# A large network on one core: merge gates sent through DRAM, an attention head's scores moved ahead of splits, and recurrent rows gated in two halves

## The chip, the cores and the metric

The kernel runs on one core of one Trainium2 chip. A core has TensorE (matmuls and transposes; PE in the profile, with weight loads listed as PEld), VectorE (DVE), ScalarE (ACT), GpSimd (POOL) and SyncE (SP), and DMA engines that the queues of SP, ACT and POOL feed. Each engine works through its own instructions in order. The metric is the time of one execution in microseconds, the median of three runs.

## The reference

A sequence of 512 tokens of width 1024 goes through two blocks. The first has two layers: a dilated sliding-window attention (three groups of windows, eight heads each, whose outputs are mixed by their log-sum-exp) and a gated linear recurrence, each followed by a convolutional feed-forward layer. The second block has two layers with three branches each, merged by gates:

```python
# one head of the first attention: three groups g, mixed by alpha
o = jnp.sum(jax.nn.softmax(jnp.stack(lses), axis=0)[..., None] * jnp.stack(outs), axis=0)
# recurrent layer
gate = jax.nn.gelu(gb, approximate=True)
_, hs = lax.associative_scan(_lru_combine, (a, b), axis=1)
return (hs * gate) @ w_out
# second block, per layer
h = _rmsnorm(x, norm_g[l]); z = h @ w_in[l]
o_a = nsa(...) * silu(nsa_silu); o_b = fox(...) * silu(fox_silu); o_m = memory(...) * silu(mem_silu)
g = jax.nn.sigmoid(merge_g).reshape(B, T, 3, D)
u = g[:, :, 0] * (o_a @ w_branch_a) + g[:, :, 1] * (o_b @ w_branch_b) + g[:, :, 2] * (o_m @ w_branch_m)
x = x + u @ w_out[l]
```

Here nsa is an attention with a compressed, a selected and a windowed part, fox an attention with forget gates, and memory a cross-attention to 256 memory rows.

## The kernel before

Every number is fp32. A matrix operand is split into a high and a low part (a cast on ACT, then a subtraction on DVE: `split`, L204), and a product is three matmuls, high x high, high x low, low x high (`mm3`, L45 to L47). Weights come by `wunit`: a load on SP's queue into one of two `ws` tiles, then a split into one of four pairs `wh`, `wl`. PSUM banks are handed out by tag: three `acc`, two `sc`, two `tr`, one `pv`.

The kernel is written in a framework in which each tile belongs to a tag with a fixed number of buffers; its scheduler orders each engine's instructions, in general by program order among those that are ready. `issue_after(ins)` (wrapped by `behind`) queues what is written inside it behind `ins`, on the engine of `ins` alone.

First attention (`dilated_attention`): for each of eight heads, six feature blocks of the query/key projection are computed (orders 1 and 0 of the tokens for different groups), scores, exponentials, a pair of statistics per order (`W`). The two orders exchange statistics through DRAM: L112 writes this order's, L113 reads the other's. `normalize` combines them (DVE, ACT, then POOL scales the rows), and `values` transposes the scaled rows (tags PA, PB; L143, L154) and multiplies them with the values. For the last head these two run inside `hold`, between the first seven eighths and the last eighth of the output projection's first half (`tm`). The projection's left operand is the split of oT, one split for each head.

Recurrent layer (`lru_layer`): `LRU_STEPS` writes out an order. An integer n is `front(n)` (convolution, gate matrices, tanh for rows 2n and 2n+1), a range is `recur` (the decay exponentials and the scan for these rows), and each "v" copies one of eight raw gate blocks from its bank to a tile on DVE. At the end, every row m gets its Gelu (from the raw copy, or straight from the bank for the rest), is multiplied with it and split for the output projection.

Second layers (`second_layer`): memory, nsa and fox are generators; `weave` runs one of them and, after the steps listed in `PLANS`, calls a filler generator once. nsa and fox have 40 steps each, memory 20. The filler is `branch`: for each of eight column blocks m a gate (24 matmuls, in two calls, then a tanh into a tile `mt`) and a product o @ w_branch (12 matmuls), multiplied with (1 + tanh) into u by DVE and, for the second and third branch, added to u by POOL (L1043, L1046, L1047). The gate of m + 1 comes before the product of m. The tag `st` has seven buffers of [128, 2048] fp32, which hold keys, values, queries and the two u tiles.

Of the kernel before, what the change touches and what calls it, by code (L numbers as in the profile page):

```python
# [28 lines left out]
SEC_BUFS = {"st": 7, "ws": 2, "w": 4, "o": 6, "P": 5, "pt": 4, "zc": 3, "hst": 4, "fox_t": 4, "of": 2, "rt": 2, "sl": 2, "mt": 2, "cst": 2, "ct": 2}  # L29
LRU_BUFS = 24  # L30
NORMALIZE_AFTER, VALUES_AFTER = 5, 6
LRU_STEPS = (0, 1, 2, range(4), "v", 3, range(4, 8), "vvv")
PLANS = ((16,),
         (8, 13, 13, 14, 15, 18, 19, 19, 22, 22, 25, 26, 26, 27, 27, 28, 28, 29, 29, 35, 35, 37, 38, 39),
         (1, 5, 5, 8, 8, 10, 12, 15, 16, 17, 19, 21, 32, 32, 34, 35, 38))
# [24 lines left out]
class DilatedHead:  # L60
# [23 lines left out]
    def scores(self, qk, order):  # L84
        n, nc = self.n, self.n.nc
        own = self.W[:, order, 0]
        ps = None
        for t in range(NT):
            ts = slice(t * 128, (t + 1) * 128)
            P = self.rows(order, t)  # L90
            N = P.shape[-1]
            if order:

                S = n.bank("sc").rearrange("p (g u c) -> p u g c", g=2, u=2)
                for g in (1, 2):
                    q = qk[g]
                    nc.tensor.matmul(S[:, :, g - 1], q[:, 0, ts], q[:, 2:4, ts], start=True, stop=False)
                    nc.tensor.matmul(S[:, 0, g - 1], q[:, 1, ts], q[:, 2, ts], start=False, stop=True)
                two = lambda x: x.rearrange("p (g c) -> p g c", g=2)
                nc.vector.tensor_tensor(two(P), S[:, 1], two(self.bias[:, 256:512]), op=OP.add)  # L100
                S, bias, P3 = S[:, 0], two(P), two(P)
            else:
                if t % 2 == 0:
                    ps = n.bank("sc")
                S = ps[:, t % 2 * 256:t % 2 * 256 + N]
                q, ks = qk[0], slice((t + 1) * 128 - N, (t + 1) * 128)
                mm3(nc, S, q[:, 0, ts], q[:, 1, ts], q[:, 2, ks], q[:, 3, ks], True, True)
# [61 lines left out]
class Net:  # L169
# [287 lines left out]
    def dilated_attention(self, qkv, oT):  # L457
# [54 lines left out]
        a.scores(qk, 0)  # L512
# [6 lines left out]
        return last  # L519
# [26 lines left out]
    def attn_layer(self, g_next, nxt):  # L546
        i, tc = self.i, self.tc
        with tc.tile_pool(name="attO", bufs=1) as self.op, tc.tile_pool(name="attA", bufs=2) as self.ap:
# [4 lines left out]
            last = self.dilated_attention(self.attn_qkv(self.h), oT)  # L553
# [135 lines left out]
    def lru_layer(self, lin, g_next, nxt):  # L689
        nc, i, tc = self.nc, self.i, self.tc  # L690
        with tc.tile_pool(name="lru", bufs=1) as lp:
# [63 lines left out]
            raw = 0  # L755
            for step in LRU_STEPS:
                if isinstance(step, int):
                    front(step)
                elif isinstance(step, str):
                    for e in step:  # L760
                        (nc.scalar.copy if e == "a" else nc.vector.tensor_copy)(gate[:, raw], next(lin))
                        raw += 1
                else:
                    last_y = recur(step)
            for m in range(KD):
                x, g = xs[m // 2], gate[:, m]
                ps = g if m < raw else next(lin)
                with self.tc.issue_after(last_y.ins):
                    nc.scalar.activation(g, ps, AF.Gelu_apprx_tanh)  # L769
                nc.vector.tensor_tensor(hs[m], hs[m], g, op=OP.mult)  # L770
                self.split(x[0][:, m % 2], x[1][:, m % 2], hs[m])
# [137 lines left out]
    def pv(self, ps, first, last, v, pts, half):  # L909
# [3 lines left out]
        for j in range(nj):  # L913
            lo = 128 if j == nj - 1 else 0
            for u, p in enumerate(pts):
                nc.tensor.matmul(ps[:, lo:256], v(j), p[:, j, lo:], start=first and j == 0 and u == 0, stop=last and j == nj - 1 and u == 1)  # L916
# [40 lines left out]
    def second_layer(self, l, z2):  # L957
        nc, i, tc = self.nc, self.i, self.tc
        w_in, h = i["w_in_2"][l], self.h
        with tc.tile_pool(name=f"sec{l}", bufs=1) as self.lp:  # L960
            lp = self.lp
            u, o_m, o_a, o_b = [], [], [], []
            br = [self.branch(l, h, o, i[f"w_branch_{x}_2"][l], b, u) for o, x, b in ((o_m, "m", 2), (o_a, "a", 0), (o_b, "b", 1))]
            self.weave(self.memory(l, h, w_in, z2, o_m), br[0], PLANS[0])
            self.weave(self.nsa(l, h, w_in, o_a), itertools.chain(br[0], br[1]), PLANS[1])
            self.weave(br[0])
            self.weave(self.fox(l, h, w_in, o_b), itertools.chain(br[1], br[2]), PLANS[2])
            self.weave(br[1])
            self.weave(br[2])
# [38 lines left out]
    def branch(self, l, h, o, w, b, u):  # L1008

        nc = self.nc  # L1010
        kt = 4
        wv = w.rearrange("(k p) c -> p k c", p=128)
        first = not u
        ts = []

        wg = self.i["w_in_2"][l].rearrange("(k p) c -> p k c", p=128)

        def gate(m):
# [9 lines left out]
            ts.append(t)  # L1028
            yield

        yield from gate(0)
        for m in range(KD):
            if m + 1 < KD:
                yield from gate(m + 1)
# [507 lines left out]
```

## Time and profile before

| | |
|---|---|
| median of three runs (2843.86 to 2845.45) | 2844.17 us |
| the profiled execution | 2847.33 us |
| its span, first to last instruction | 2845.2 us |
| TensorE busy | 2752.4 us, 14493 matmuls |
| DVE busy | 1655.0 us |
| ACT busy | 1285.5 us |
| POOL busy | 509.2 us |
| mean granted clock of TensorE | 0.988 |
| DMA | 288.52 MB, 101 GB/s from and to HBM over the span |

Times in views count from the span's start. A row of windows gives an engine's busy time in a stretch; the rest of the stretch it was idle. PEclk is the granted clock of TensorE as a share of full speed; it has two levels, 1.0 (2.4 GHz) and 0.5 (1.2 GHz), and a value between them is a mean over the stretch.

### The profile page before, as it was taken

What the parts mean: (1) busy time and instruction counts of PE and PEld (TensorE: products, weight loads), DVE (VectorE), ACT (ScalarE), POOL (GpSimd) and SP (SyncE); (2) the same over time, 40 slices, a digit from 0 to 9 for tenths busy, and PEclk for the clock granted to TensorE, in tenths of its full rate; (3) what the DMA queues carried; (4) which work ended last, traced back from release to release, by engine and by line L of the source; (5) the groups of instructions that cost most, each with busy time, mean ns of one, the idle gap of its engine ahead of it and who ended that gap; (6) DMA issues with size and microseconds to landing.
All of it is one profiled execution on the core that took longest, in us unless ns stands there. A gap on an engine that the chain in (4) does not pass through costs nothing.

```text
span 2845.2 us, 39405 instructions
## 1 busy us (share of the span) xinstructions
PE 2752.4 (97%) x14493; PEld 2338.7 (82%) x14493; DVE 1655.0 (58%) x3306; ACT 1285.5 (45%) x2518; POOL 509.2 (18%) x682
## 2 busy tenths in 40 slices
PE   7999999799999998999998999999999899999999
PEld 6788888688888887888887898789878798788987
DVE  3245555555542678555425687776744677777753
ACT  3234344344432465444323554666533554665542
POOL 0001101111100000111001242333320242333420
PEclk9999999899999999999999999999999999999999
DMA  5553443333332343433323424122234423113233
GB/s 172 171 169 86 104 94 86 118 111 97 97 126 96 112 122 108 126 96 97 126 97 114 125 74 109 38 54 75 71 93 141 137 70 109 34 46 84 71 93 107
DMA packets 386071, 288.52 MB, mean 101 GB/s; under 512 B 33576, under 2 KB 339496, under 8 KB 385880
## 3 DMA queue, kind: packets, MB, share of 16 engines
q1 hardware_dynamic: 376752, 268.94, 32.9%
q10 hardware_dynamic: 9128, 17.07, 1.6%
q8 instruction: 115, 1.88, 0.3%
q14 instruction: 76, 0.62, 0.1%
HBM read 266.86 MB, written 21.20 MB: 101 GB/s over the span
## 4 chain that ended last, share of the span: by engine, by line
PE 82%; DVE 8%; DMA 4%; ACT 3%; issue 2%; POOL 1%; SPq 0%; ACTq 0%; DVEq 0%; POOLq 0%
PE acc L45 20%; PE acc L46 20%; PE acc L47 20%; PE tr L856 2%; PE sc L45 2%; PE sc L46 2%; PE sc L47 2%; DVE wl L204 2%; PE pv L916 2%; PE tr L45 2%; PE tr L47 1%; PE tr L46 1%; PE pv L46 1%; PE pv L47 1%; DMA ws<-in_attn_w_qkv_dram 1%
## 5 line engine op out<-in xcount | busy, mean ns | idle before, releaser
L204 DVE TENSOR_TENSOR wl<-ws,wh 128x1024 fp32r<-128x1024 f32 (+2 forms) x476 | 563.9, 1186 | 686.8 <-ACT wh L204 680.8
L204 ACT CAST wh<-ws 128x1024 fp32r<-128x1024 f32 (+2 forms) x476 | 469.5, 987 | 819.7 <-PE acc L46 303.6
L45 PE MATMUL acc<-hH,wh 128*128 128x512 f32 (+1 forms) x1928 | 742.3, 386 | 12.2 <-ACT gate L769 6.2
L46 PE MATMUL acc<-hL,wh 128*128 128x512 f32 (+1 forms) x1928 | 741.3, 385 | 1.5 <-DVE hL L204 1.2
L47 PE MATMUL acc<-hH,wl 128*128 128x512 f32 (+1 forms) x1928 | 739.5, 384 | 1.0 <-DVE wl L204 1.0
L45 PEld LDWEIGHTS acc<-hH,wh 128*128 128x128 f32 x1928 | 363.3, 189 | 83.6 <-ACT gate L769 6.6
L47 PEld LDWEIGHTS acc<-hH,wl 128*128 128x128 f32 x1928 | 363.9, 189 | 69.2 <-DVE wl L204 1.5
L46 PEld LDWEIGHTS acc<-hL,wh 128*128 128x128 f32 x1928 | 364.1, 189 | 68.4 <-DVE hL L204 2.5
L45 PE MATMUL acc<-wh,hH 128*128 128x256 f32 (+3 forms) x864 | 267.3, 312 | 5.4 <-ACT hH L204 4.1
L46 PE MATMUL acc<-wl,hH 128*128 128x256 f32 (+3 forms) x864 | 266.9, 310 | 2.3 <-DVE wl L204 2.3
L47 PE MATMUL acc<-wh,hL 128*128 128x256 f32 (+3 forms) x864 | 264.9, 309 | 0.1
L45 PEld LDWEIGHTS acc<-wh,hH 128*128 128x128 f32 x864 | 165.6, 192 | 14.5 <-ACT hH L204 4.5
L46 PEld LDWEIGHTS acc<-wl,hH 128*128 128x128 f32 x864 | 165.7, 192 | 11.9 <-DVE wl L204 3.7
L47 PEld LDWEIGHTS acc<-wh,hL 128*128 128x128 f32 x864 | 165.3, 191 | 7.4 <-DVE hL L204 0.4
L645 POOL TENSOR_TENSOR cv<-cv 128x512 f32<-128x512 f32 x48 | 62.0, 1292 | 465.1 <-DVE cv L582 448.4
L582 DVE SCALAR_TENSOR_TENSOR cv<-acc,cw,cv 128x511 f32<-128x511 f32 (+1 forms) x192 | 142.5, 746 | 3.2
L856 PE MATMUL tr<-ident,P 128*128 128x128 f32 x720 | 123.3, 277 | 10.7 <-DVE pt L204 5.2
L817 POOL TENSOR_TENSOR hst<-hst,mhalf 128x4 f32<-128x4 f32 (+2 forms) x90 | 91.0, 1017 | 223.5 <-DVE hst L816 221.7
L889 ACT ACTIVATE P<-P,soft 128x128 f32<-128x128 f32 (+1 forms) x192 | 108.1, 563 | 49.9 <-DVE soft L888 45.7
L888 DVE CUSTOM_DVE_ANT_0 P<-sc,causal 128x128 f32<-128x128 f32 (+1 forms) x192 | 92.9, 486 | 45.8 <-PE tr L856 31.5
L891 POOL TENSOR_SCALAR P<-P,soft,ngate 128x128 f32<-128x128 f32 (+3 forms) x128 | 83.9, 658 | 153.6 <-DVE soft L890 117.5
L204 DVE TENSOR_TENSOR pt<-tr,pt 128x128 fp32r<-128x128 f32 (+2 forms) x224 | 104.1, 474 | 11.8 <-ACT pt L204 10.4
(452 smaller groups left out, 4770.1 us busy)
## 6 DMA issues: line engine op xcount, KB each, us to landing
ws<-in_w_in_dram SPq DMA_DIRECT2D x116, 512.0 KB
ws<-in_ffn_w_up_dram SPq DMA_DIRECT2D x96, 512.0 KB
ws<-in_attn_w_qkv_dram SPq DMA_DIRECT2D x72, 512.0 KB
ws<-in_ffn_w_down_dram SPq DMA_DIRECT2D x48, 512.0 KB
x<-x ACTq DMA_DIRECT2D x16, 512.0 KB
ws<-in_lru_w_in_dram SPq DMA_DIRECT2D x16, 512.0 KB
ws<-in_w_mem_kv_dram SPq DMA_DIRECT2D x16, 512.0 KB
ws<-in_w_out_dram SPq DMA_DIRECT2D x16, 512.0 KB
```

Source lines behind the costliest of these rows:

```text
L45: nc.tensor.matmul(out, lh, rh, start=start, stop=False)
L46: nc.tensor.matmul(out, lh, rl, start=False, stop=False)
L47: return nc.tensor.matmul(out, ll, rh, start=False, stop=stop)
L204: return nc.scalar.copy(hi, src), (eng or nc.vector).tensor_tensor(lo, src, hi.bitcast(F32), op=OP.subtract)
L582: nc.vector.scalar_tensor_tensor(dst[:, s:], ps[:, :T - s], cw(taps - 1 - s), dst[:, s:], op0=OP.mult, op1=OP.add)
L645: nc.gpsimd.tensor_tensor(g, g, v, op=OP.mult)
L817: nc.gpsimd.tensor_tensor(st[:, 1], st[:, 0], self.mhalf[:rows, :nh], op=OP.pow)
L856: self.nc.tensor.transpose(ps[:, a * 128:(a + 1) * 128], s, self.ident)
L888: nc.vector.tensor_tensor_reduce(out=P, in0=S, in1=self.causal[:, 512 - n:512], scale=-1.0, scalar=BIG, op0=OP.add, op1=OP.min, accum_out=m)
L889: nc.scalar.activation(P, P, AF.Exp, bias=m, scale=-1.0, accum_out=s)
L891: nc.gpsimd.tensor_scalar(P, P, r, mult, op0=OP.mult, op1=OP.mult)
L916: nc.tensor.matmul(ps[:, lo:256], v(j), p[:, j, lo:], start=first and j == 0 and u == 0, stop=last and j == nj - 1 and u == 1)
```

## The change

It has three parts. In the first attention, the last head's order-0 scores return their last reduction and last exponential, and the first seven splits of oT queue behind them on DVE and ACT; the last head's read of the other order's statistics is issued by POOL instead of SP; and its normalization queues behind the seventh split alone, no longer behind the last weight split too. In the recurrent layer, five gate blocks instead of four are copied raw, in another order, rows 0 to 3 get their Gelu, multiplication and split between the two recurrences (`finish(0, 4)`), and the second recurrence's exponentials queue behind the last of these Gelus. In the second layers, a branch's gates become a generator of their own (`gates`), whose tanh results ACT stores to DRAM; `branch` loads them back, one block ahead; the filler is one chain over gates and products of m, a and b with new plans; four calls of it queue their matmuls behind the last value matmul of fox; and the tag mt has three buffers.

```diff
-SEC_BUFS = {"st": 7, "ws": 2, "w": 4, "o": 6, "P": 5, "pt": 4, "zc": 3, "hst": 4, "fox_t": 4, "of": 2, "rt": 2, "sl": 2, "mt": 2, "cst": 2, "ct": 2}
+SEC_BUFS = {"st": 7, "ws": 2, "w": 4, "o": 6, "P": 5, "pt": 4, "zc": 3, "hst": 4, "fox_t": 4, "of": 2, "rt": 2, "sl": 2, "mt": 3, "cst": 2, "ct": 2}
-LRU_STEPS = (0, 1, 2, range(4), "v", 3, range(4, 8), "vvv")
-PLANS = ((16,),
-         (8, 13, 13, 14, 15, 18, 19, 19, 22, 22, 25, 26, 26, 27, 27, 28, 28, 29, 29, 35, 35, 37, 38, 39),
-         (1, 5, 5, 8, 8, 10, 12, 15, 16, 17, 19, 21, 32, 32, 34, 35, 38))
+LRU_STEPS = (0, 1, 2, range(4), "vv", 3, "vv", (0, 4), range(4, 8), "v")
+PLANS = ((3, 3, 3, 3, 16, 16),
+         (8, 8, 12, 13, 14, 16, 18, 19, 20, 21, 22, 23) + tuple(range(24, 40)),
+         (1, 5, 8, 10, 12, 13, 14, 15, 16, 17, 18, 19, 21, 25, 28, 30, 32, 33, 34, 35, 36, 37, 38, 39))
...
-            nc.vector.tensor_tensor_reduce(out=P3, in0=S, in1=bias, scale=-1.0, scalar=BIG, op0=OP.add, op1=OP.min,
-                                           accum_out=own[:, 0, t:t + 1])
-            nc.scalar.activation(P, P, AF.Exp, bias=own[:, 0, t:t + 1], scale=-1.0, accum_out=own[:, 1, t:t + 1])
+            ends = (nc.vector.tensor_tensor_reduce(out=P3, in0=S, in1=bias, scale=-1.0, scalar=BIG, op0=OP.add, op1=OP.min,
+                                                   accum_out=own[:, 0, t:t + 1]),
+                    nc.scalar.activation(P, P, AF.Exp, bias=own[:, 0, t:t + 1], scale=-1.0, accum_out=own[:, 1, t:t + 1]))
         nc.sync.dma_start(self.in_dram(order, order), own)
-        nc.sync.dma_start(self.W[:, 1 - order, 1], self.in_dram(order, 1 - order))
+        (nc.gpsimd if self.hd == 7 else nc.sync).dma_start(self.W[:, 1 - order, 1], self.in_dram(order, 1 - order))
+        return ends
...
-            for k in range(KD - 1):
-                done = self.split(oh[0][:, k], oh[1][:, k], oT[:, k])
+            with behind(tc, *ends):
+                for k in range(KD - 1):
+                    done = self.split(oh[0][:, k], oh[1][:, k], oT[:, k])
 
             def hold():
-                last((*done, *self.last_split))
+                last(done)
...
-                    nc.scalar.activation(a, r, AF.Exp, scale=l4[:, m:m + 1], bias=l4[:, m:m + 1])
+                    with behind(tc, gelu[-1]):
+                        nc.scalar.activation(a, r, AF.Exp, scale=l4[:, m:m + 1], bias=l4[:, m:m + 1])
...
+            def finish(lo, hi):
+                for m in range(lo, hi):
+                    x, g = xs[m // 2], gate[:, m]
+                    ps = g if m < raw else next(lin)
+                    with behind(tc, last_y):
+                        gelu.append(nc.scalar.activation(g, ps, AF.Gelu_apprx_tanh))
+                    nc.vector.tensor_tensor(hs[m], hs[m], g, op=OP.mult)
+                    self.split(x[0][:, m % 2], x[1][:, m % 2], hs[m])
...
+                elif isinstance(step, tuple):
+                    finish(*step)
...
-            for m in range(KD):
...
+            finish(4, KD)
...
-            br = [self.branch(l, h, o, i[f"w_branch_{x}_2"][l], b, u) for o, x, b in ((o_m, "m", 2), (o_a, "a", 0), (o_b, "b", 1))]
-            self.weave(self.memory(l, h, w_in, z2, o_m), br[0], PLANS[0])
-            self.weave(self.nsa(l, h, w_in, o_a), itertools.chain(br[0], br[1]), PLANS[1])
-            self.weave(br[0])
-            self.weave(self.fox(l, h, w_in, o_b), itertools.chain(br[1], br[2]), PLANS[2])
-            self.weave(br[1])
-            self.weave(br[2])
+            self.gd = self.dp.tile([3, KD, 128, T], F32, name=f"gd{l}")
+            fill = itertools.chain.from_iterable(
+                (f for b, (o, x) in enumerate(((o_m, "m"), (o_a, "a"), (o_b, "b")))
+                 for f in (self.gates(l, h, (2, 0, 1)[b]), self.branch(o, i[f"w_branch_{x}_2"][l], (2, 0, 1)[b], u))))
+            self.weave(self.memory(l, h, w_in, z2, o_m), fill, PLANS[0])
+            self.weave(self.nsa(l, h, w_in, o_a), fill, PLANS[1])
+            self.weave(self.fox(l, h, w_in, o_b), fill, PLANS[2])
+            with behind(tc, self.last_pv):
+                for n in range(4):
+                    next(fill)
+            self.weave(fill)
...
             t = self.lt("mt", [128, T])
             nc.scalar.activation(t, pg, AF.Tanh, scale=0.5)
-            ts.append(t)
+            nc.scalar.dma_start(self.gd[b, m], t)
             yield
...
+        def load(m):
+            t = self.lt("mt", [128, T])
+            nc.sync.dma_start(t, self.gd[b, m])
+            return t
+
+        ts = [load(0)]
         for m in range(KD):
             if m + 1 < KD:
-                yield from gate(m + 1)
+                ts.append(load(m + 1))
```

## Rows read from the trace of the kernel before

**Rows 1.** The page, busy time of each engine: us, share, instructions.

```profile
PE   2752.4 (97%) x14493; PEld 2338.7 (82%) x14493; DVE 1655.0 (58%) x3306; ACT 1285.5 (45%) x2518; POOL 509.2 (18%) x682
```

**Rows 2.** Windows at the attention's end: busy us by engine, clock, DMA share, GB/s.

```profile
480.80:487.00 6.20, 6.20 (x29) 5.12 (x29) 6.20 (x14) 5.14 (x12) 0.00 (x0) 1.00 0.02 2
...
507.90:515.00 7.10, 0.13 (x1) 0.00 (x0) 2.26 (x8) 1.16 (x2) 0.40 (x2) 0.72 0.47 153
515.00:527.80 12.80, 9.16 (x43) 7.68 (x43) 4.98 (x8) 3.44 (x6) 3.17 (x7) 0.63 0.45 152
527.80:532.40 4.60, 4.55 (x13) 3.61 (x14) 0.69 (x1) 0.52 (x2) 0.00 (x0) 0.60 0.34 139
```

**Rows 3.** The chain in order of time, 490 to 530: start, us, what.

```profile
496.00 9.64 DMA dx<-W
...
506.11 5.19 DMA ws<-in_attn_w_o_dram
511.38 1.05 ACT wh L204
512.46 1.23 DVE wl L204
```

**Rows 4.** Timeline of ACT, then DVE, at the attention's end: start, us, instruction.

```profile
479.44 2.17 ACT L204 CAST hH<-oT 128x512 fp32r<-128x512 f32 x4
...
495.38 0.49 ACT L111 ACTIVATE PA<-PA,W 128x256 f32<-128x256 f32 x1
...
509.74 0.17 DVE L122 TENSOR_TENSOR c<-W 128x8 f32<-128x8 f32 x1 [4.08 <-DMA W<-dx]
```

**Rows 5.** Windows at the end of the recurrent layer.

```profile
1070.00:1076.70 6.70, 0.49 (x4) 0.06 (x2) 6.52 (x10) 6.67 (x12) 0.00 (x0) 0.81 0.19 59
1076.70:1081.10 4.40, 4.40 (x11) 3.48 (x12) 4.40 (x9) 4.40 (x8) 0.00 (x0) 0.51 0.29 108
...
1102.70:1131.20 28.50, 27.30 (x124) 22.08 (x123) 17.03 (x31) 12.20 (x24) 3.63 (x5) 1.00 0.22 74
```

**Rows 6.** Timelines of ACT, PE and DVE in the recurrent layer.

```profile
1072.67 1.28 ACT L769 ACT_TABLE_LOAD   x1
1073.97 0.63 ACT L769 ACTIVATE gate<-gate 128x512 f32<-128x512 f32 x1
...
1076.69 0.79 PE L45 MATMUL acc<-hH,wh 128*128 128x512 f32 x1 [6.21 <-ACT gate L769]
...
1101.94 1.46 DVE L204 TENSOR_TENSOR xl<-th,xh 128x512 fp32r<-128x512 f32 x2
```

**Rows 7.** Windows in the two second layers.

```profile
1775.00:1811.50 36.50, 30.65 (x197) 24.42 (x195) 32.12 (x125) 31.00 (x94) 17.88 (x29) 1.00 0.08 21
1880.00:1900.00 20.00, 17.42 (x109) 14.39 (x108) 17.24 (x65) 14.03 (x42) 9.67 (x13) 1.00 0.01 2
...
2088.00:2096.00 8.00, 5.71 (x22) 4.30 (x21) 2.50 (x4) 1.96 (x3) 0.00 (x0) 0.79 0.46 154
2098.00:2142.00 44.00, 44.00 (x193) 35.86 (x193) 22.49 (x25) 15.87 (x24) 9.27 (x6) 1.00 0.38 108
2431.00:2467.00 36.00, 31.45 (x189) 26.09 (x188) 29.55 (x116) 28.54 (x85) 16.71 (x27) 0.91 0.06 15
2538.00:2556.00 18.00, 15.26 (x87) 12.52 (x85) 14.38 (x56) 11.38 (x35) 9.45 (x13) 0.91 0.01 2
...
2740.00:2752.00 12.00, 9.57 (x42) 7.46 (x41) 4.76 (x8) 3.50 (x6) 0.55 (x1) 0.86 0.31 109
```

**Rows 8.** Timelines of PE and DVE where the long stretch ends.

```profile
1810.29 0.39 PE L1161 MATMUL sc<-st 128*128 128x512 f32 x1
...
1810.82 1.27 DVE L1043 SCALAR_TENSOR_TENSOR st<-mt,acc 128x512 f32<-128x512 f32 x2
```

**Rows 9.** The chain in order of time, 1560 to 1600: a weight load.

```profile
1575.22 4.01 DMA ws<-in_w_mem_kv_dram
```

**Rows 10.** Line 400, DMA issues on ACT's queue: ns min/median/max.

```profile
L400 ACTq DMA_DIRECT2D x<-x x16: 326/326/327, 541.7 to 1539.2; - x16
```

More of the change, by code (lines that the diff above doesn't have):

```diff
@@ L511, in dilated_attention @@
                 after(VALUES_AFTER, values, a)
-        a.scores(qk, 0)
+        ends = a.scores(qk, 0)
         due(True)
@@ L518, in last @@
             values(a)
-        return last
+        return last, ends
     def first_rows(self, g):
@@ L552, in attn_layer @@
             oT = self.op.tile([128, KD, T], F32, tag="oT", bufs=1, name="oT")
-            last = self.dilated_attention(self.attn_qkv(self.h), oT)
+            last, ends = self.dilated_attention(self.attn_qkv(self.h), oT)
             oh = self.new_h()
-            for k in range(KD - 1):
-                done = self.split(oh[0][:, k], oh[1][:, k], oT[:, k])
+            with behind(tc, *ends):
+                for k in range(KD - 1):
+                    done = self.split(oh[0][:, k], oh[1][:, k], oT[:, k])
             def hold():
-                last((*done, *self.last_split))
+                last(done)
                 self.split(oh[0][:, KD - 1], oh[1][:, KD - 1], oT[:, KD - 1])
@@ L753, in recur @@
                 return last
-            raw = 0
+            raw, gelu = 0, [None]
+            def finish(lo, hi):
[6 more added lines that the diff above has]
+                    self.split(x[0][:, m % 2], x[1][:, m % 2], hs[m])
             for step in LRU_STEPS:
@@ L762, in lru_layer @@
                         raw += 1
+                elif isinstance(step, tuple):
+                    finish(*step)
                 else:
                     last_y = recur(step)
-            for m in range(KD):
[L766 to L771, printed above, removed]
+            finish(4, KD)
             lh = lambda k, t: xs[k // 2][0][:, k % 2, t * 128:(t + 1) * 128]
@@ L915, in pv @@
             for u, p in enumerate(pts):
-                nc.tensor.matmul(ps[:, lo:256], v(j), p[:, j, lo:], start=first and j == 0 and u == 0, stop=last and j == nj - 1 and u == 1)
+                self.last_pv = nc.tensor.matmul(ps[:, lo:256], v(j), p[:, j, lo:], start=first and j == 0 and u == 0, stop=last and j == nj - 1 and u == 1)
     def merge_halves(self, of, ps, e, half):
@@ L1006, in second_layer, with gates @@
             return gen
-    def branch(self, l, h, o, w, b, u):
+    def gates(self, l, h, b):
         nc = self.nc
[L1011 to L1014, printed above, removed]
         wg = self.i["w_in_2"][l].rearrange("(k p) c -> p k c", p=128)
-        def gate(m):
+        for m in range(KD):
             c = OFF_MG + b * D + m * 128
@@ L1027, in gate, with branch @@
             nc.scalar.activation(t, pg, AF.Tanh, scale=0.5)
-            ts.append(t)
+            nc.scalar.dma_start(self.gd[b, m], t)
             yield
-        yield from gate(0)
+    def branch(self, o, w, b, u):
+        nc = self.nc
+        kt = 4
+        wv = w.rearrange("(k p) c -> p k c", p=128)
+        first = not u
+        def load(m):
[3 more added lines that the diff above has]
+        ts = [load(0)]
         for m in range(KD):
             if m + 1 < KD:
-                yield from gate(m + 1)
+                ts.append(load(m + 1))
             wh, wl = self.wunit(wv[:, :, m * 128:(m + 1) * 128])
```

## The prediction

> **What bounds the kernel now.** I read the engine lines of the page first, then TensorE's waits, then the chain in order of time, and last windows around each place where TensorE stood still. TensorE is busy for 97% of the span [rows 1]: the kernel is bound by matmuls. No product is added or removed, so the change can win only two things, TensorE's idle time (2845.2 - 2752.4 = 92.8 us) and time in which the granted clock was at the lower of its two levels. I count the second as (1 - granted clock) x busy time of a window. An edit is worth what it takes from these two in its own stage.
>
> There are three such stages. At the end of the attention, TensorE idles 7.10 - 0.13 = 6.97 us in 507.9 to 515, another 12.80 - 9.16 = 3.64 us in 515 to 527.8, and runs at 0.63 and 0.60 of the clock until 532.4, which costs 0.37 x 9.16 + 0.40 x 4.55 = 5.2 us [rows 2]. The chain names the cause: the last head's statistics leave at 496.00 and take 9.64 us to land, and then a weight load (5.19 us), its cast and its subtraction (1.05 and 1.23 us) stand in it [rows 3]. In the recurrent layer TensorE waits 6.21 us for the Gelu that frees a bank [rows 6], and then has 0.51 of the clock for 4.40 us, which costs 2.2 us [rows 5]. In the two second layers there are bare stretches [rows 7]: attention heads without filler (36.50 - 30.65 = 5.85 us idle; 36.00 - 31.45 = 4.55 us and 0.09 x 31.45 = 2.8 us of clock), the last heads of the first branch (2.58; 2.74 and 0.09 x 15.26 = 1.4), and the end of the forget branch (2.29 and 0.21 x 5.71 = 1.2; 2.43 and 0.14 x 9.57 = 1.3).
>
> **Part 1, last head's scores first.** The seven splits of oT now queue behind the last head's reduction and exponential, the read of the other order's statistics moves from SP's queue to POOL's, and the normalization no longer queues behind a weight split. Before, ACT runs four oT casts from 479.44 (2.17 us) ahead of the last query split, and the last exponential starts at 495.38 [rows 4]. Without these casts, and with DVE and ACT free of seven splits, I estimate that it ends near 486 (bounds 484 and 492). Then the write lands at 486 + 9.64 = 495.6. A read issued by POOL is in no row; the nearest is the same read issued by SP, for which DVE waited 4.08 us [rows 4]; with that, it lands at 499.7. Nothing on POOL is held up by waiting for it: behind it stands only the last normalization, which needs it. From the landing at 509.74 to the idle end at 515.0 before were 5.3 us; without the cast and subtraction in front (2.3 us) 3.0 are left: the normalized rows are there at 502.7, before TensorE's present work runs out (507.9). So the 6.97 us and the 5.2 us of clock go: 12.2. The new price: the 29 matmuls that stand in 480.8 to 487 [rows 2] are the first of the output projection, and they need the splits, which now start at 486. What hides this is head 6's transposes and value products, which have to run anyway. I take half of the 6.2 us as uncovered, 3, and the gain as **9** (bounds 1: nothing covered, clock as before; 16: all covered, and the 3.64 us woven in as well).
>
> **Part 2, rows 0 to 3 gated between the recurrences.** One more gate is copied raw, so that three rather than four wait in the three banks: the wait of 6.21 us has no place any more, and its 2.2 us of clock go with it. Against this, ACT switches tables twice more, 1.28 us each, as the load at 1072.67 shows [rows 6], and the second recurrence's exponentials stand behind four Gelus, which stand behind two more raw copies on a full DVE (6.52 of 6.70 us busy) [rows 5]. That delays rows 4 to 7. How much of it reaches the end: DVE splits row 7 at 1101.94 to 1103.4 [rows 6], and TensorE ends the projection at 1131.2, 28.5 us after the 1102.7 where I start that window [rows 5]. What really needs row 7 is 12 matmuls of the first half and 75 of the second, 87 x 0.228 = 19.8 us (0.228 from 44.00 us for 193 matmuls [rows 7]). So 8.7 us are slack, in which the 8.4 us can be taken, less what row 7 comes later. I put that at 4 and the gain at **4** (bounds -3: row 7 comes 11 us later; 8: no later).
>
> The next activation starts 0.02 us after that load has ended [rows 6]. The Trainium skill (ScalarE: Activation LUTs, "What ACT_TABLE_LOAD costs") counts a drain of about 1.38 us on top of a load of 1.28 us, 2.66 per switch; by that the two switches would take 5.3 us instead of 2.6, and this gain would be 1.3. The trace does not agree, as no such pause follows the load.
>
> **Part 3, gates through DRAM.** 48 tanh results of 256 KB go out by ACT's queue and come back by SP's. The order of the 72 fillers of a layer changes: all gates of a branch, then its products. After the last step of the forget branch 14 are left (3 gates, 8 products) instead of 30, and the first four of them, 48 matmuls = 10.9 us, queue behind its last value matmul.
>
> End of the forget branch: these 10.9 us cover the waits of 2.29 and 2.43 us, and the clock has no reason to fall: 2.29 + 1.2 + 2.43 + 1.3 = **7** (their weights may load earlier: only matmuls queue behind a matmul). Last heads of the first branch: fillers had run out there; now gates of the next product are ordered one half to a step: of 2.58 + 2.74 + 1.4 = 6.7 I take **6** (bounds 0 and 7).
>
> The long bare stretch (1775 to 1811.5 and 2431 to 2467; 5.85 + 4.55 + 2.8 = 13.2 us) I leave as it is, **0**. Two products of branch m end it at 1810.82, right after a score matmul at 1810.29 [rows 8]: their sums go to the second u tile, one state tile more than the seven slots hold, which waits for the first query tile. The new order asks for that tile at step 26 instead of 28, and the waiting products then hold banks and the three mt tiles just as gates and products did before. Bounds 0 and 13.
>
> The price: 48 issues on ACT at 0.326 us [rows 10], beside matmuls except where ACT is itself nearly full (31.00 of 36.50 us [rows 7]): **-1** (bounds 0 and -5). At the end of a layer eight products stand in a row, 12 x 0.228 = 2.74 us each, and each wants 256 KB of weights and 256 KB of gate. That is 191 GB/s, where 108 GB/s kept the DMA engines 0.38 busy [rows 7], so bandwidth holds (0.67). Latency: two staging tiles, each 4.01 us for a load of 512 KB [rows 9], 1.05 and 1.23 us of splitting [rows 3], give a unit every 3.1 us at worst, 0.4 too slow, 16 times = 6.5 us; a unit of 256 KB is shorter: **-2** (bounds 0 and -6.5). The added bytes, 25 MB over some 1280 us, are 20 GB/s.
>
> Sum: 9 + 4 + 7 + 6 + 0 - 1 - 2 = **23 us**. It is made against the span of 2845.2; the profiled execution took 2847.3, and the median of the three runs is 2844.2. So 2822 in the span, and **2821** as a median.
>
> **Rivals.** (a) Neither front stage pays: TensorE idles for all of 480.8 to 487 and its clock still falls, and row 7 comes 11 us later. Then 1 - 3 replaces 9 + 4: 2836. For it: the splits do start later, DVE is full. Against: the slack, head 6's work. (b) The long bare stretch fills, because gates no longer hold mt tiles until their product: 2821 - 13 = 2808. Against it: the u tile still waits. (c) The spread does not take place: what fills one stretch is missing in the next, so that the 7 and 6 of part 3 are lost, and (a) holds as well, in all within 2 us of nothing: 2844, no change. (d) Slower: the eight bare products are set by a gate row's return. Place: the last 22 us of each layer's merge, 16 products. If SP can issue a row only when a mt tile is freed, a product takes a whole load and the work that frees the tile, some 4.01 + 1.2 = 5.2 us (1.2 estimated from the subtraction in rows 3) instead of 2.74: 16 x 2.5 = 40 us, 2861. It decides from 2.74 + 23/16 = 4.2 us a product, a little over one whole load. Against it: three mt tiles, each asked for one product ahead.
>
> **How the numbers follow.** Forecast 0.48 (its own range 2811 to 2832), (a) 0.17, (b) 0.17, (c) 0.08, (d) 0.10. 0.2% is 5.7 us, about what a measurement can tell from no change. Faster: 0.48 + 0.17 + 0.14 of (a) = 0.79; same: 0.07 of (c) and 0.03 of (a) = 0.10; slower: (d) and the rest, 0.11. The range leaves out (d), the worse half of (c), and (b) with part 1 at its best: 2800 to 2843.
>
> **What would show it.** Part 1: W's write near 486, no wait at PA's transposes, the clock whole through 532. Part 2: no wait on the Gelu of a bank, row 7's split no later than 1107 in the old count. Part 3: no wait on o at the two branch ends, filler in the last heads, u's fifth row still right after the first query tile's last score. Wrong would be: products spaced over 4 us at a layer's end, or a new low clock where the output projection waits for its splits.

## The result: slower by 0.7%, and where the profile after puts it

The changed kernel takes 2865.05 us (median of 4 runs, 2862.22 to 2868.06), the kernel before 2844.02 (4 runs, 2843.22 to 2845.45). The ratio is 1.0074, 95% interval 1.0056 to 1.0091: some 21 us slower, where 23 us faster was forecast. The profiled execution took 2868.06 us, its span is 2866.1 us. The engines' line on the page of the changed kernel, to set beside [rows 1]:

```profile
PE   2765.0 (96%) x14493; PEld 2348.5 (82%) x14493; DVE 1650.5 (58%) x3307; ACT 1292.7 (45%) x2520; POOL 523.0 (18%) x684
```

The same 14493 matmuls are busy for 12.6 us longer, at a mean granted clock of 0.983 instead of 0.988, and the idle time is 101.1 instead of 92.8 us. To see which stage lost it, I took the instructions that mark the ends of stages from TensorE's timeline, first of the kernel before, then of the one after (start, us, instruction):

```profile
548.69 0.60 PE L320 MATMUL acc<-ident,spare 128*128 128x128 f32 x4
...
1125.54 0.60 PE L320 MATMUL acc<-ident,spare 128*128 128x128 f32 x4
...
2180.23 0.60 PE L320 MATMUL acc<-ident,o 128*128 128x128 f32 x4
...
2840.96 0.39 PE L47 MATMUL tr<-wh,st 128*128 128x512 f32 x1
```

```profile
545.34 0.60 PE L321 MATMUL acc<-ident,spare 128*128 128x128 f32 x4
...
1129.42 0.60 PE L321 MATMUL acc<-ident,spare 128*128 128x128 f32 x4
...
2194.26 0.60 PE L321 MATMUL acc<-ident,o 128*128 128x128 f32 x4
...
2861.78 0.39 PE L47 MATMUL tr<-wh,st 128*128 128x512 f32 x1
```

The changed kernel is 3.3 us ahead behind the attention, 3.9 behind after the recurrent layer, 14.0 behind after the first of the two second layers and 20.8 behind at the end. So the attention's end gained 3.3 us, the recurrent layer lost 7.2, and the second layers lost 10.2 and 6.8 us (next to nothing happens between the stages). What such a difference is worth can be read from the traces of the experiments below, in the stages that an experiment leaves as they were. There the attention's mark lies between 544.7 and 552.9 us, the recurrent layer's comes 575.7 to 577.1 us later (584.1 in the changed kernel), and the two second layers, without the stage ahead of them, take 618.6 to 621.9 and 661.4 to 665.0 us (630.7 and 671.8). The three losses are clear of that spread; the 3.3 us of the attention are not.

**Attention's end.** Timelines of ACT, POOL, DVE and PE (to set beside [rows 2 to 4]):

```profile
490.50 0.49 ACT L111 ACTIVATE PA<-PA,W 128x256 f32<-128x256 f32 x1
...
501.54 0.72 POOL L113 DMA_DIRECT2D W<-dx  x1 [12.28 <-DMA dx<-W]
...
504.74 0.17 DVE L123 TENSOR_TENSOR c<-W 128x8 f32<-128x8 f32 x1 [7.75 <-DMA W<-dx]
...
511.06 0.93 PE L144 MATMUL tr<-ident,PA 128*128 128x128 f32 x7
...
512.41 1.23 DVE L205 TENSOR_TENSOR wl<-ws,wh 128x1024 fp32r<-128x1024 f32 x1 [3.64 <-ACT wh L205]
...
512.81 0.38 PE L45 MATMUL pv<-ptA,vH 128*128 128x256 f32 x1 [0.82 <-ACT ptA L205]
...
514.16 0.53 PE L46 MATMUL pv<-ptA,vH 128*128 128x256 f32 x1 [0.97 <-DVE ptA L205]
...
520.83 0.36 PE L163 MATMUL pv<-ptB,vH 128*128 128x256 f32 x1 [1.46 <-DVE oT L167]
...
524.62 0.79 PE L45 MATMUL acc<-wh,hH 128*128 128x512 f32 x1 [2.05 <-ACT hH L205]
```

The last exponential starts 4.9 us earlier than before, and the transposes of PA no longer wait. The windows show the rest:

```profile
480.00:487.00 7.00, 4.82 (x27) 4.47 (x26) 4.85 (x11) 3.57 (x10) 0.00 (x0) 0.76 0.23 77
...
515.00:524.60 9.60, 6.00 (x33) 5.45 (x31) 3.73 (x7) 2.38 (x4) 0.00 (x0) 0.68 0.60 203
524.60:529.00 4.40, 4.38 (x13) 3.49 (x14) 0.69 (x1) 0.50 (x2) 0.00 (x0) 0.62 0.35 142
```

In 480 to 487 TensorE now idles 2.2 us and has 0.76 of the clock; and behind PA the last head's own chain (cast, subtraction, sum) leaves short waits of 0.82, 0.97, 1.46 and 2.05 us, and the granted clock of these stretches is 0.68 and 0.62, where it was 0.63 and 0.60. The wait of 0.97 us stands behind a weight's subtraction (512.41): the weight split that no longer holds up the normalization now holds up the step after it.

**Recurrent layer.** Timelines of ACT, PE and DVE (to set beside [rows 6]):

```profile
1057.29 0.69 DVE L205 TENSOR_TENSOR xl<-xb,xh 128x512 fp32r<-128x512 f32 x1
...
1066.92 0.70 ACT L724 ACTIVATE th<-sc,lruhb 128x512 f32<-128x512 f32 x1
1067.63 1.28 ACT L733 ACT_TABLE_LOAD   x1
...
1085.95 1.28 ACT L766 ACT_TABLE_LOAD   x1
1087.25 0.63 ACT L766 ACTIVATE gate<-gate 128x512 f32<-128x512 f32 x1
...
1088.42 0.79 PE L45 MATMUL acc<-wh,xh 128*128 128x512 f32 x1 [10.42 <-ACT gate L766]
...
1106.99 1.47 DVE L205 TENSOR_TENSOR xl<-th,xh 128x512 fp32r<-128x512 f32 x2
```

The wait of 6.21 us for a Gelu has not gone: it is 10.42 us, now of the output projection, and row 7's split comes 5 us later although the layer began 3.3 us earlier. The second recurrence's first table load (1067.63) stands right behind the last gate tanh (1066.92). That tanh needs the last front's split, which ends at 1057.98; in the kernel before it ended at 1046.85:

```profile
1046.16 0.69 DVE L204 TENSOR_TENSOR xl<-xb,xh 128x512 fp32r<-128x512 f32 x1
```

**Second layers.** Windows (to set beside [rows 7]), the last two lines in the second layer:

```profile
1700.00:1800.00 100.00, 91.78 (x553) 77.84 (x551) 68.72 (x182) 44.70 (x99) 28.90 (x43) 0.95 0.42 120
...
1801.50:1835.50 34.00, 29.75 (x190) 24.11 (x189) 27.39 (x103) 26.10 (x78) 14.76 (x24) 1.00 0.11 31
1904.00:1926.00 22.00, 22.00 (x160) 20.79 (x160) 15.14 (x45) 13.99 (x35) 5.99 (x9) 1.00 0.26 73
...
2100.00:2116.00 16.00, 12.77 (x63) 10.38 (x63) 9.89 (x25) 8.29 (x21) 1.77 (x3) 0.76 0.31 100
2116.00:2156.00 40.00, 40.00 (x170) 32.32 (x168) 18.91 (x24) 12.73 (x20) 10.91 (x7) 0.97 0.47 145
...
2562.00:2582.00 20.00, 20.00 (x148) 18.92 (x147) 12.40 (x40) 11.26 (x31) 5.29 (x8) 1.00 0.13 36
...
2762.00:2778.00 16.00, 12.71 (x64) 10.37 (x64) 9.80 (x26) 8.30 (x21) 1.77 (x3) 0.76 0.30 100
```

The last heads of the first branch (1904 to 1926 and 2562 to 2582) have no idle time and the whole clock. The bare products at the layer's end (2116 to 2156) run without a pause. But two places are worse. The end of the forget branch idles 3.2 us and loses 0.24 x 12.77 = 3.1 us by the clock, 6.3 in place of 3.5 us. And the 100 us from 1700, where the first branch prepares its heads, lose 8.2 us idle and 0.05 x 91.78 = 4.6 us by the clock; the same stretch of the kernel before (1685 to 1785) had 2.6 us idle and 1.00:

```profile
1685.00:1785.00 100.00, 97.36 (x604) 82.76 (x602) 74.14 (x195) 49.75 (x112) 29.94 (x45) 1.00 0.36 99
```

What stands still there, and at the forget branch's end, in the changed kernel (timelines of PE and DVE):

```profile
1724.76 1.00 PE L45 MATMUL acc<-wh,hH 128*128 128x256 f32 x3 [2.47 <-ACT wh L205]
...
1749.41 0.50 PE L45 MATMUL acc<-o,wh 128*128 128x512 f32 x1
...
1775.83 1.05 PE L1268 MATMUL sc<-KC,st 128*128 128x64 f32 x8 [2.47 <-DVE P L1271]
...
1780.29 1.88 DVE L1063 SCALAR_TENSOR_TENSOR st<-mt,acc 128x512 f32<-128x512 f32 x3
...
2105.48 0.30 PE L866 MATMUL tr<-ident,P 128*128 128x128 f32 x1 [1.29 <-DVE pt L205]
...
2111.95 2.48 PE L926 MATMUL pv<-pt,st 128*128 128x256 f32 x8 [0.68 <-ACT pt L205]
```

The first product starts at 1749.41, but its sum is formed at 1780.29 together with the next two. From 1768.48, when the third starts, until then three products hold the three acc banks, and no further filler can start in TensorE's pauses.

### The profile page after: what moved, and what is told of

It is laid out like the page before. It is cut to its first block, busy times and chain, and to the rows that moved or that the text cites. A ratio compares the mean times of both kernels' runs of the same rounds, so it can differ in the third digit from the quotient of the medians.

```text
span 2866.1 us, 39570 instructions
## 1 busy us (share of the span) xinstructions
PE 2765.0 (96%) x14493; PEld 2348.5 (82%) x14493; DVE 1650.5 (58%) x3307; ACT 1292.7 (45%) x2520; POOL 523.0 (18%) x684
## 4 chain that ended last, share of the span: by engine, by line
PE 84%; DVE 6%; ACT 3%; DMA 3%; issue 2%; POOL 1%; SPq 0%; ACTq 0%; POOLq 0%; DVEq 0%
PE acc L45 21%; PE acc L46 21%; PE acc L47 20%; PE tr L866 3%; PE pv L926 2%; PE sc L45 2%; PE sc L46 2%; PE sc L47 2%; DVE wl L205 2%; PE tr L45 1%; PE tr L47 1%; PE tr L46 1%; ACT wh L205 1%; PE pv L46 1%; PE pv L47 1%
## 5 line engine op out<-in xcount | busy, mean ns | idle before, releaser
L205 DVE TENSOR_TENSOR wl<-ws,wh 128x1024 fp32r<-128x1024 f32 (+3 forms) x476 | 565.2, 1189 | 718.7 <-ACT wh L205 713.4
L205 ACT CAST wh<-ws 128x1024 fp32r<-128x1024 f32 (+3 forms) x476 | 469.6, 987 | 794.8 <-PE acc L46 295.5
```

Source lines behind the costliest of these rows:

```text
L205: return nc.scalar.copy(hi, src), (eng or nc.vector).tensor_tensor(lo, src, hi.bitcast(F32), op=OP.subtract)
```

## The experiments

Each was timed beside the kernel before on its own chip; "over" and "under" are (ratio - 1) x that chip's median, with the interval behind it. The kernel before had medians of 2840.7, 2847.8, 2844.0 and 2847.2 us in the four sets, so only the differences are compared.

### The parts alone

Parts 1, 2 and 3 of the diff above, each alone on the kernel before.

> Part 1 alone on the kernel before. Theory S (each part has the effect that its own stage shows in the trace of the changed kernel, and the parts don't touch each other): the first transposes of the next layer came 3.4 us earlier there (545.3 after 548.7), so 2840 to 2841, with the 7 us wait for PA gone and the low clock behind it still there. Rival R (the predicted terms hold for each part alone, and the parts spoil each other): 9 us faster, 2835.

> Part 2 alone on the kernel before. Theory S: the recurrent layer lost 7.2 us in the trace of the changed kernel (3.3 us ahead at its start, 3.9 us behind at its end), so 2851, with a wait of some 10 us on the Gelu of a bank. Rival R: 4 us faster, 2840, and no such wait.

> Part 3 alone on the kernel before. Theory S: the two second layers lost some 10 and 7 us in the trace of the changed kernel, so 2861. Rival R: 10 us faster (7 + 6 - 1 - 2), 2834.

Part 1: ratio 0.9995 (0.9986 to 1.0005), 1.4 us under (4.0 under to 1.4 over). Part 2: 1.0019 (1.0010 to 1.0029), 5.4 over. Part 3: 1.0068 (1.0053 to 1.0083), 19.3 over. Together 23 us, near the whole change's 21: the parts don't spoil each other, and theory R falls for all three. Part 1 alone can't be told from no change. In the profiles its stage (first score of the last head to the transposes) takes 73.9 us in the changed kernel, 70.4 in part 1 alone and 72.7 in the last version below, and 75.0 to 80.0 in the twelve traces with the old code (77.3 in the kernel before). So the stage did get shorter, but a single trace doesn't say by how much, and 0 to 5 us is as close as I can put it.

### Part 3: the trip or the order

The gates go through DRAM with three mt tiles, with the old order and the old steps, and no call is queued behind the last value matmul (the edit to `branch`, against the changed kernel):

```diff
-        ts = [load(0)]
+        ts = []
+        yield from self.gates(l, h, b, (0,))
         for m in range(KD):
+            ts.append(load(m))
             if m + 1 < KD:
-                ts.append(load(m + 1))
+                yield from self.gates(l, h, b, (m + 1,))
```

> Part 3's trip through DRAM alone: each gate's tanh goes out by ACT's queue and comes back by SP's, three mt tiles, but gates and products in the old order (gate m+1, product m), at the old steps, and nothing queued behind the last value matmul. Theory O (the loss of the second layers comes from the new order of the fillers): within 5 us of the kernel before, 2841 to 2849. Rival D (it comes from the trip: 48 stores on ACT, 48 loads on SP's queue in front of the weights): most of the loss is here too, 2854 or more.

Measured: ratio 0.9975 (0.9966 to 0.9985), 7.1 us under (9.7 to 4.3). The trip costs nothing that shows; it gains. The 26 us between this run and part 3 alone belong to the order, with its steps and its four queued calls. The gain sits at the end of the forget branch, as its windows there show (2.29 us idle and 0.79 before [rows 7]); the two rows of the timeline say what fills it:

```profile
2075.00:2091.00 16.00, 15.86 (x79) 13.13 (x78) 5.89 (x11) 5.01 (x10) 0.00 (x0) 1.00 0.59 181
2735.00:2751.00 16.00, 16.00 (x75) 13.19 (x74) 8.27 (x12) 6.07 (x10) 3.15 (x3) 1.00 0.59 182
```

```profile
2083.81 0.45 PE L45 MATMUL acc<-hH,wh 128*128 128x512 f32 x1
...
2089.32 0.63 PE L45 MATMUL acc<-o,wh 128*128 128x512 f32 x2
```

Between the last value matmul (to 2083.97) and the first product that needs o (2089.32) stand the 24 matmuls of one more gate.

Is it the third mt tile that came with the trip? The kernel before with `"mt": 3` alone:

> The kernel before with a third mt tile and nothing else, no trip through DRAM. Theory M (the old order through DRAM gained 6 us because a third mt tile lets one more gate run ahead of the wait for o): about as fast as that run, 6 us under the kernel before. Rival N (the trip itself does it: a gate's tile comes free once its store has landed, so any number of gates can run ahead of their products): within 2 us of the kernel before.

Measured: 1.0029 (1.0017 to 1.0042), 8.3 us over. Theory M falls, and the rival's "within 2 us" was missed as well: one more gate runs ahead, but before the last value matmul and not behind it, and the product then waits longer for o at the end of the forget branch (3.21 us in either layer, where it was 2.29):

```profile
2759.86 0.79 PE L45 MATMUL acc<-o,wh 128*128 128x512 f32 x1 [3.21 <-ACT o L204]
```

So more room without the trip does not help; why it costs as much as 8 us I did not follow up.

### Part 3: the two losses of the order

The four fillers behind the last value matmul, set free (on part 3 alone):

```diff
-            with behind(tc, self.last_pv):
-                for n in range(4):
-                    next(fill)
             self.weave(fill)
```

The first u tile takes its slot before the second query tile's:

```diff
+        self.u.append(self.state([128, 4, T], F32))
+        nc.gpsimd.memset(self.u[0][:, 0, 0:1], 0.0)
         QT[1] = self.state([128, 4, T])
...
-        first = not u
+        first = len(u) < 2
...
-                if m % 4 == 0:
+                if m // 4 == len(u):
                     u.append(self.state([128, 4, T], F32))
```

> Part 3 alone, but the four fillers at the end of the forget branch are not queued behind its last value matmul. Theory Q (held back there, they leave the branch's last heads bare; the granted clock falls for 10 us at 2102 and 2764 in the run of part 3 alone): the waits and the low clock there go, 4 to 5 us for each layer, so 8 to 10 us faster than part 3 alone, some 10 us over the kernel before. Rival L (the last heads' own chain of exponential and cast sets the pace, fillers or not): within 3 us of part 3 alone.

> Part 3 alone, but the first u tile takes its state slot before the second query tile (one element is set to zero by GpSimd, which every product's sum then overwrites). Theory U (slots are given in the order of first writes; behind PTC's, u's comes so late that three products hold the three acc banks for 20 us while TensorE runs bare into the compressed scores): the first sum is there some 20 us earlier, and 5 us a layer come back, 10 us faster than part 3 alone. Rival W (that stretch is set by the weights that come late and by the chain of the compressed scores): within 3 us of part 3 alone.

> Part 3 alone with both mends: fillers not queued, first u tile early. Theory U with Q: the two add, 18 to 20 us faster than part 3 alone, the time of the kernel before, with the late weights ahead of the compressed scores still there (4 us in the first layer). Rival L with W: within 5 us of part 3 alone.

Measured: fillers set free 1.0018 (1.0008 to 1.0027), 5.1 us over; early u tile 1.0040 (1.0025 to 1.0055), 11.4 over; both 0.9992 (0.9983 to 1.0002), 2.3 under, no difference from the kernel before. Against part 3's 19.3 these give back 14, 8 and 22 us. Q and U hold, and they add; Q gave more than the 8 to 10 us that it said. The windows of the run with free fillers, at its two branch ends, are full at the whole clock; behind them a wait of 1.54 us for o, which the queued fillers had covered, is back in either layer (the second fence is the same place in part 3 alone):

```profile
2101.00:2117.00 16.00, 16.00 (x85) 13.43 (x84) 8.16 (x20) 7.98 (x18) 1.30 (x3) 1.00 0.22 67
...
2761.00:2777.00 16.00, 16.00 (x85) 13.54 (x84) 5.24 (x10) 5.68 (x13) 0.19 (x1) 1.00 0.33 99
...
2126.71 0.96 PE L45 MATMUL acc<-o,wh 128*128 128x512 f32 x3 [1.54 <-ACT o L204]
```

```profile
2095.00:2111.00 16.00, 12.85 (x63) 10.48 (x63) 9.88 (x25) 8.29 (x21) 1.77 (x3) 0.76 0.30 100
```

With the early u tile the first sum comes at 1757.10, 9 us after its product began (1747.72) and not 31; windows of that run:

```profile
1715.00:1731.00 16.00, 13.38 (x86) 12.14 (x83) 10.01 (x18) 6.74 (x14) 2.41 (x5) 0.79 0.54 148
1755.00:1771.00 16.00, 16.00 (x78) 12.83 (x77) 10.82 (x26) 6.14 (x14) 0.00 (x0) 1.00 0.68 203
...
1787.00:1803.00 16.00, 11.13 (x42) 8.12 (x42) 9.92 (x36) 9.16 (x25) 5.84 (x11) 0.82 0.25 66
```

1755 to 1771 is full now, but 1787 to 1803 is barer than in part 3 alone (14.24 us busy there): part of what is won is only moved to the start of the long stretch, I take it because the fillers are used up sooner. The first window, with the late weights at 1722, is left as it was; that cause I did not test.

### Part 2: three theories

Other banks for the output projection, and the last front put ahead of three raw copies (each on part 2 alone):

```diff
-        y0 = [gained(t, 0, y) for t, y in enumerate(list(self.tm(w, 0, 512, lh, ll, kt=kt, banks=2 if hold else 0, hold=hold)))]
+        y0 = [gained(t, 0, y) for t, y in enumerate(list(self.tm(w, 0, 512, lh, ll, kt=kt, banks=2 if hold else tb[0], hold=hold)))]
...
-        y1 = self.tm(w, 512, 512, lh, ll, kt=kt, banks=3 if hold else 1, tail=4, after=self.last_pe if hold else None)
+        y1 = self.tm(w, 512, 512, lh, ll, kt=kt, banks=3 if hold else tb[1], tail=4, after=self.last_pe if hold else None)
```

```diff
-LRU_STEPS = (0, 1, 2, range(4), "vv", 3, "vv", (0, 4), range(4, 8), "v")
+LRU_STEPS = (0, 1, 2, range(4), "v", 3, "vvv", (0, 4), range(4, 8), "v")
```

(`tb` is (1, 2) in the recurrent layer and (0, 1) elsewhere: rows of TOK_BANKS, the list of banks by token tile.)

> Part 2 alone, but the recurrent layer's output projection takes the sc and tr banks for its first half, which are free since the last tanh of the gates, and the acc banks for its second half. Theory K (the 10.4 us wait is a collision of banks: the first half asks for the three acc banks in which the gates 5 to 7 wait for their Gelu): the wait goes and the layer is back at the old time or better, 6 us or more faster than part 2 alone. Rival Z (rows 4 to 7 are late, and the projection needs them soon after): the wait goes from the Gelu of a bank to the splits of rows 4 to 7, and the time stays within 3 us of part 2 alone, which was 5 to 6 us over the kernel before.

> Part 2 alone, but with the last front right behind the first raw copy, as before the change: the steps are 0, 1, 2, the first recurrence, one copy, 3, three copies, the Gelus of rows 0 to 3, the second recurrence, one copy. Theory Z (the layer loses because the second recurrence starts late, 5.4 us of it by the raw copy that stands ahead of front 3): 4 to 6 us faster than part 2 alone, at the time of the kernel before. Rival G (it loses by the two more table switches and the Gelus between the recurrences): within 2 us of part 2 alone.

Measured: other banks 1.0032 (1.0020 to 1.0044), 9.1 us over; front earlier 1.0028 (1.0017 to 1.0040), 8.0 over; part 2 alone was 5.4 over (2.8 to 8.2). Theory K, the obvious reading of the 10.42 us, falls (Z's "within 3 us of part 2 alone" is missed by 0.7, well inside the intervals): with free banks TensorE waits for weights (behind the same busy ACT) and for rows instead:

```profile
1092.22 0.80 PE L45 MATMUL acc<-wh,xh 128*128 128x512 f32 x1 [4.82 <-ACT wh L204]
...
1103.23 0.79 PE L45 MATMUL sc<-wh,xh 128*128 128x512 f32 x1 [3.39 <-ACT xh L204]
```

The front put earlier did not bring its 4 to 6 us either. In its trace the projection ends 3.6 us earlier than in part 2 alone (table below), but three stages that the edit doesn't touch are 2.5 to 3.2 us longer each, so the times can't show it. The last gate tanh runs there 78 us after the layer's first convolution instead of 94, but the second recurrence's first table load comes only at 88, right behind the fourth Gelu. That led to theory H, and two more versions on part 2: five raw copies and no early Gelu, and two rows gated early.

```diff
-LRU_STEPS = (0, 1, 2, range(4), "vv", 3, "vv", (0, 4), range(4, 8), "v")
+LRU_STEPS = (0, 1, 2, range(4), "v", 3, range(4, 8), "vvvv")
...
-            finish(4, KD)
+            finish(0, KD)
```

```diff
-LRU_STEPS = (0, 1, 2, range(4), "vv", 3, "vv", (0, 4), range(4, 8), "v")
+LRU_STEPS = (0, 1, 2, range(4), "v", 3, "v", (0, 2), range(4, 8), "vvv")
...
-            finish(4, KD)
+            finish(2, KD)
```

> The kernel before with five gates copied raw instead of four, and all Gelus after the second recurrence as before; nothing gated between the recurrences. Theory H (part 2 loses because the second recurrence stands behind four Gelus, and these behind four gates' matmuls and copies, 5.4 us each on TensorE, where one stood ahead of it before): the second recurrence has its old time, row 7's last split starts some 125 us after the layer's first convolution (125.5 before, 134 in part 2 alone), and the time is within 2 us of the kernel before; the 6.2 us for the bank only become a wait for the rows. The prediction's own step (the fifth copy takes that wait away for good): 4 to 6 us faster.

> Part 2 alone, but rows 0 and 1 only are gated between the recurrences: the steps are 0, 1, 2, the first recurrence, one copy, 3, one copy, Gelus of rows 0 and 1, the second recurrence, three copies, the rest. Theory H: two gates' units stand ahead of the second recurrence instead of four, so it starts some 10 us earlier than in part 2 alone, row 7's last split starts at 127 to 130 after the layer's first convolution, and the time lies 3 to 6 us under part 2 alone, within 3 us of the kernel before. Rival G (the two more table switches and the Gelus in between cost it, which this version keeps): as slow as part 2 alone, 5 us or more over the kernel before.

Measured: five copies 1.0004 (0.9994 to 1.0013), 1.1 us over (1.7 under to 3.7 over); two rows 1.0017 (1.0008 to 1.0026), 4.8 over (2.3 to 7.4): H's "within 3 us" is missed, and by the time alone G is nearer. The traces say more than the times. All are counted in us from the layer's first convolution (976.47 before, 973.13 after):

| version | table load for the second recurrence's Ln | row 7's split ends | start of the projection's last matmul but one | from the split to it |
|---|---|---|---|---|
| before | 86.8 | 126.9 | 154.3 | 27.4 |
| five copies | 87.0 | 127.0 | 154.3 | 27.3 |
| two rows early | 89.0 | 126.3 | 156.3 | 30.0 |
| front earlier | 98.5 | 131.6 | 158.8 | 27.2 |
| changed kernel | 104.5 | 135.3 | 161.5 | 26.2 |
| part 2 alone | 105.0 | 135.8 | 162.4 | 26.6 |
| other banks | 104.5 | 135.3 | 162.1 | 26.8 |

With one exception the layer is longer by about as much as row 7's split is late, and that split is late where the second recurrence is. Two rows early are the exception: they keep the table switches, split row 7 on time (earlier than H said) and lose 2.0 us, with two waits of 2.19 and 3.06 us for the split of the projection's weights. Four rows lose 7 to 8: by the traces the late second recurrence explains the larger part, and G has some 2 us; that the timed run puts two rows at 4.8 leaves G's share open. With five copies 1.35 us of the wait for a bank are left, the first wait is now for a row's split (3.28 us), and the layer has its old length to 0.1 us.

### What gained, put together

Part 1 and the trip with the old order; the recurrent layer as before.

> A version put together from what gained: part 1, and part 3's trip through DRAM with the fillers in the old order at the old steps; the recurrent layer as before. If the two add (1 us and 7 us in their own runs): 8 us faster than the kernel before, ratio 0.997. If part 1 is worth nothing by itself: 0.9975. Rival: the fox branches' gain was an accident of one order of instructions and goes when the stages ahead shift: within 2 us of the kernel before.

Measured: 2834.43 against 2844.01 us, ratio 0.9969 (0.9957 to 0.9981), 8.8 us under (12.2 to 5.4). That is what the two would give together, though the interval doesn't tell it from the trip alone, and this version beats both kernels. Its forget branches are full in both layers (16.00 of 16.00 us, clock 1.00, at 2080 and at 2740).

## Why the prediction was wrong, step by step

**Part 1, forecast 9, measured 0 to 5.** Each link held, though some 5 us later than forecast: the last exponential within its bounds (490.5; estimate 486), the write's landing (10 us), the read by POOL (issued in 0.72 us, W used 3.2 us after its start, less than the 4.08 I took), no wait at PA. What failed is "so the 6.97 us and the 5.2 us of clock go". The 6.97 us went, but the last head's own chain put 0.82 + 0.97 us in their place; and of the 5.2 us 0.32 x 6.00 + 0.38 x 4.38 = 3.6 stayed, for the short waits are there without the long one, and so is the low clock. And 480 to 487 cost 2.2 us idle and 1.2 us of clock, not far from my 3. Of the 12.2 that leaves 12.2 - 1.8 - 3.6 - 3.4 = 3.4 us, what the marks of the two traces give.

**Part 2, forecast +4, measured -5 in the timed run and -7 in the trace.** Two terms failed, and a step is missing. The first is "the wait of 6.21 us has no place any more": three waiting gates fill three banks, so the projection waited for one, and five copies alone, which cut that wait to 1.35 us, win nothing, because the wait for a bank only stood in front of the wait for rows. The second is the slack of 8.7 us. I had counted 87 matmuls that really need row 7. But TensorE's queue holds the second half token by token: in the trace before, 24 matmuls of rows 6 and 7 and 84 of the second half stand behind row 7's split, 108 x 0.228 = 24.6 us and some waits, and the last matmul follows that split by 26 to 27 us in all but one version. There is no slack, so nearly each us by which row 7 is late is lost, and it was late by 8.4, not by 4. What made it late is a step that the prediction doesn't have. It let the second recurrence wait for four Gelus; but in the changed kernel the fourth Gelu runs 79.0 us after the first convolution, and the second recurrence starts at 94.5, behind the last front's tanh (93.8; 75.9 before). One more gate's matmuls stand ahead of that front's convolutions, which start 6.6 and 8.1 us later (with the front put earlier they are back in place), and its last split, then among the first recurrence's multiplications on DVE, ends 14.5 us later. Only with the front put earlier is the fourth Gelu (87.8) what holds the second recurrence, and it follows the fourth copy (85.1): that is the chain of theory H. The table loads were priced rightly: 1.28 us each, and the next activation 0.02 us after the last one's end (1087.25). The Trainium skill (ScalarE: Activation LUTs, "What ACT_TABLE_LOAD costs") would put a drain of 1.38 us beside each; this trace again shows none.

**Part 3, end of the forget branch, forecast +7, measured -5 to -8** (6.3 against 3.5 us, and 6.3 against 2.43 + 1.3 = 3.7; and 0.03 x 40 = 1.2 us of clock behind each). The step "these 10.9 us cover the waits of 2.29 and 2.43 us, and the clock has no reason to fall" looked at the waits behind the last value matmul and not at the heads ahead of it. Fillers that must stay behind that matmul are no cover for what comes before it. There DVE and ACT set the pace (waits of 1.29 and 0.68 us, and one of 0.86 between them), and the granted clock of these 16 us is 0.76. The waits for o were covered, as forecast. Setting the fillers free gave 14 us back; the windows and the low clock behind them, 6.3 + 1.2 in either layer, less the wait of 1.54 us for o that came back, make 12 of them.

**Last heads of the first branch, forecast +6:** right; their idle time and low clock are gone. **Layer's end, forecast -2:** 40.00 us of 40 busy, 96 products' matmuls in 22.6 us, 2.82 us a product. Rival (d), decided at 4.2, does not take place. **The long bare stretch, forecast 0:** right for the stretch itself (34.0 - 29.75 = 4.25 us idle), and u's fifth row came behind it as before.

**The stretch ahead of it, not in the sum, measured -10 in the first layer.** This is the largest miss. I followed the u tile of the fifth row and forgot that of the first. Before, the first product was asked for at step 14, ahead of the second query tile and PTC; in the new order all sixteen gate calls come first, so u's first tile stands behind both in the order in which slots are given. The products meanwhile held the acc banks "just as gates and products did before" only in my text. Giving the tile an early place brought 8 us back in two layers (by the marks of the traces some 4 in the first and 6 in the second). So in the first layer it explains less than half of the 10: the late weights (2.6 us idle and 2.8 us of clock in that run) remain, and part of the rest moved into the long stretch.

So in place of 9 + 4 + 10 = 23 the parts measure 0 to 5, -5 to -7, and -19. Of the rivals (d) is nearest in number, 2861, and that is luck: what it describes did not happen. Rival (c), that what fills one stretch is missing in the next, is nearest in kind, but it too lost the 6 us of the last heads, which were won, and it had neither the late second recurrence nor the tile.

## What to carry to other kernels

Reordering fillers also reorders the tiles and banks they take: for each filler that moves, ask which tile it takes first, behind which other tiles it now stands, and what its unfinished result holds while it waits. A wait taken away is worth only what the next wait lets through, so find that one first; and slack must be counted with the queue's order, not with what each matmul needs. Cover for a stretch has to be free to run in it: work queued behind the stretch's end helps only afterwards.

## What the runs showed of the hardware

A round trip of 48 x 256 KB out by ACT's queue and back by SP's, 25 MB added in all, costs no time that shows; with the old order it won 7 us. And short waits in a row were followed by the lower clock as one long wait was: at the attention's end the wait of 7.0 us went, but with waits of 0.82, 0.97, 1.46 and 2.05 us the windows there still had 0.68 and 0.62 of the clock.
